# A two-layer hybrid attention step on one core: waits moved in seven stages, and column sums of layer 0 taken on 64 rows per head and divided by quarters

## The chip, the core and the metric

The kernel runs on one core of a Trainium2 chip. The metric is the device time of one execution in microseconds (us). A core has five engines with a queue of instructions each, which run in the order of their queue: TensorE (PE in the rows, with PEld for its weight loads), VectorE (DVE), ScalarE (ACT), GpSimd (POOL) and SyncE (SP, which issues transfers here). Data lie in SBUF and results of matmuls in PSUM, which this kernel uses as eight banks of 128 partitions by 512 floats.

## The reference

Two residual layers are computed for one prompt of 128 tokens and for one sample of 1024 tokens with 1024 channels. Each layer is the same frame around a mixer:

```python
h = pre_norm(x, g_pre, mod)              # rms norm, scale and shift from silu(cond) @ w_mod
y = mixer(h)                             # h @ w_in, branches, gates, concat, @ w_out
x = x + mod[2] * rms_norm(y, g_post)
```

Layer 0 has attention with 8 query heads and 2 key heads of 64 channels (branch A, keys of 128 cached tokens and the sample's 1024), and means over windows of tokens (branch B):

```python
q, k = axial_rope(rms_norm(q)), axial_rope(rms_norm(k))
p = softmax(q @ concat([ctx_k, k]).T * 64 ** -0.5)        # 1152 keys
o_a = p @ concat([ctx_v, v])
y = concat([o_a * silu(ga), pool(u) @ b_map * silu(gb)]) @ w_out
```

Layer 1 has attention over a neighbourhood of tokens plus the cache (branch C, 8 heads) and attention with latent keys and values (branch D, 8 heads, 96 channels for scores: `qd = rms_norm(cq) @ w_uq`, `kv = ckv_all @ w_ukv`), gated and joined in the same way. The outputs are both residual streams and the prompt's keys, values and latents.

## The kernel before

All instructions are written out in order in Python; no scheduler moves them. What decides the order is `weave` (L27): it takes a list of main steps and a list of fill steps, each with a cost in ns that the author gave, runs the main steps in turn, and puts in a fill step whenever the share of fill cost issued lags behind the share of main cost (times `frac`). A step issues all its instructions at once, on several engines. `merge` mixes two fill lists.

Products of float32 are made from two parts: a rounded high part (`whi`, `hTh`, `KH`, made by ACT) and the rest (`wlo`, `hTl`, `KL`, made by DVE or POOL as a subtraction from the same source). PSUM has two pools of banks: three banks A (scores) and five banks B (everything else; `kn.B`, `kn.C`). A matmul that begins a new group waits for a free bank, that is, for the engine which reads the group that lay there.

The stages are these, in order of time:

- The q projection of layer 0 (some 71 to 143 us). `q_main(0)` and `q_main(1)` are its two halves of 256 columns: groups of 48 matmuls in a bank `qkv`, each followed by `q_evac` (squares on ACT, reduction, reciprocal, product and rotation on DVE and POOL). Beside the first half go the keys: `kv1` (norm), `kv2` (rotation) and `kv3` (transposes into a bank `kT`, high part by ACT casts, low part by DVE subtractions) for key groups 0 and 1 (512 tokens each) and 2 (prompt and cache). The shift and scale of layer 1 (`modps`) lie there too.
- The gates and the B branch: twelve weight chunks, each loaded, split into `whi`/`wlo`, and multiplied in a bank `gate`. `pool_mixer` makes the window means `ps` on POOL and DVE, and ACT takes their high part `dh`.
- Attention A: sixteen units in the whole kernel have the form of class `Unit`, eight of them here (four pairs of heads by two halves of 512 queries) and eight in D. A unit first needs the row maxima: 24 matmuls `mp` (`mpiece`), each reduced by DVE (`mx`), one reduction `ms`, eight 1-row matmuls `mT` which turn `ms` into rows (`mrows`), and copies of these rows by ACT into one partition of `QM`. Then for nine key tiles kt and two heads: scores `st`, exponentials `P` by ACT, sums of `P` over key tiles `acc` by POOL (DVE in the last unit of A), and products `pv` in groups after kt 3, 5 and 8 and at the start of the next unit. `fin` ends a unit during the next one: gate times `pv`; `ColSums` makes the column sums `sum` (four matmuls on 32 rows), reciprocals of two halves `srow` (DVE), their two parts `Rhl` (ACT, then DVE), a spread to all rows `rb` by matmuls, and DVE multiplies the gated values `oT` by `rb`. `run_units` weaves the units: the main list is the scores, with the last unit's end and `side` steps at given kt; the fill is the next unit's maxima and the preparation of the unit after (`prep`, with `split_heads`: ACT high part `QP`, DVE low part, ACT copy `QM`, all read from one bank `qT`).
- The output projection of layer 0 with the norms of layer 1 (`outproj`), then attention C (eight heads; `k_split` makes keys `cKH`, `cKL`; the scores `cS` lie in banks A and are read by a DVE operation whose rows bear the name `cmx`), attention D (weights `uq`, `uk` loaded per pair of heads and split; prompt steps `dk`, `dsp`), and the output projection of layer 1.

## Time and profile before

| what | value |
|---|---|
| median of 3 runs (lowest to highest) | 1601.55 us (1599.77 to 1605.28) |
| the profiled execution's own time | 1600.49 us |
| its span, first to last instruction | 1598.7 us |
| mean granted TensorE clock, as a share of 2.4 GHz | 0.980 |
| PE busy | 1518.5 us, 95% |
| DVE busy | 793.5 us, 50% |
| ACT busy | 649.4 us, 41% |
| POOL busy | 625.0 us, 39% |
| DMA queue of the loads, share of 16 engines | 21.7% |

The busy times are sums over one execution of one core. The span is the profile's own measure from the first to the last instruction, and the execution's time has 1.8 us more around it. In rows of the timeline the first number is the start in us from the span's start, the second how long the row's instructions took from the first one's start to the last one's end, and the square bracket at the end tells how long the engine was idle before the row and who released it.

### The profile page before, as it was taken

To read this page: it belongs to the slowest core of one execution; us is meant where nothing else is said; L and a number is where in the kernel's file an instruction comes from. 1 tells how busy PE (TensorE), PEld (TensorE's weight loads), DVE (VectorE), ACT (ScalarE), POOL (GpSimd) and SP (SyncE) were. 2 spreads that over 40 slices of the span, in tenths; PEclk is the share of its full clock that TensorE was granted. 3 is DMA by queue.
4 is the path that set the end of the run, shared out by engine and by line. 5 is a ranking of instruction groups with operands and counts; after the bars stand their busy time and mean duration, and the time that the engine had idled before them with its cause. 6 is when DMAs were issued, how large, how long until landed. Compare 5 with 4: busy or idle time off the path is not lost. (4 is left out here: it accounts for less than half of the span.)

```text
span 1598.7 us, 23592 instructions
## 1 busy us (share of the span) xinstructions
PE 1518.5 (95%) x9095; PEld 1238.9 (77%) x9095; DVE 793.5 (50%) x1776; ACT 649.4 (41%) x1379; POOL 625.0 (39%) x499
## 2 busy tenths in 40 slices
PE   7989999989899999899999999999999999899998
PEld 5978998945555588898989898999976656565786
DVE  4565233357575555534354443423574555546633
ACT  4332211255555323445454544444454434444311
POOL 1743212058669323641303103001256556556421
PEclk8989999999999999999999999999999999999999
DMA  9352104120001232410403130131000000013241
GB/s 343 91 195 81 40 27 145 45 100 14 1 14 40 66 106 80 87 39 15 98 16 75 39 75 24 36 100 58 1 18 21 14 27 15 21 42 117 97 147 53
DMA packets 114080, 104.81 MB, mean 66 GB/s; under 512 B 41776, under 2 KB 99952, under 8 KB 113968
## 3 DMA queue, kind: packets, MB, share of 16 engines
q1 hardware_dynamic: 113792, 103.23, 21.7%
q8 instruction: 72, 1.18, 0.3%
q14 instruction: 40, 0.33, 0.1%
q10 hardware_dynamic: 176, 0.07, 0.0%
HBM read 87.54 MB, written 15.75 MB: 65 GB/s over the span
## 5 line engine op out<-in xcount | busy, mean ns | idle before, releaser
L948 DVE TENSOR_REDUCE mx<-mp 128x1 f32<-128x384 f32 x384 | 189.1, 548 | 99.4 <-PE mp L97 98.0
L124 POOL TENSOR_TENSOR acc<-acc,P 128x1024 f32<-128x1024 f32 x84 | 199.7, 2378 | 75.0 <-ACT P L980 70.0
L980 ACT ACTIVATE P<-st 128x512 f32<-128x512 f32 x256 | 147.2, 598 | 149.1 <-PE st L97 144.1
L124 POOL TENSOR_TENSOR wlo<-raw,whi 128x1024 fp32r<-128x1024 f32 x36 | 87.5, 2433 | 266.5 <-ACT whi L113 153.2
L97 PE MATMUL yps<-whi,ohl 128*128 128x512 f32 x576 | 182.8, 393 | 0.3 <-POOL ohl L124 0.3
L97 PE MATMUL cg<-hT1h,whi 128*128 128x384 f32 x480 | 170.3, 355 | 1.9 <-DVE hf L133 1.2
L97 PE MATMUL cg<-hT1h,wlo 128*128 128x384 f32 x480 | 163.4, 341 | 1.9 <-POOL wlo L124 1.9
L97 PE MATMUL cg<-hT1l,whi 128*128 128x384 f32 x480 | 162.9, 339 | 0.0
L97 PEld LDWEIGHTS yps<-whi,ohl 128*128 128x128 f32 x576 | 108.1, 188 | 25.2 <-issue 2.4
L97 PE MATMUL yps<-wlo,ohl 128*128 128x512 f32 x288 | 112.2, 389 | 0.0
L97 PE MATMUL gate<-hTh,whi 128*128 128x384 f32 x288 | 98.1, 341 | 4.2 <-ACT whi L113 4.2
L97 PE MATMUL gate<-hTh,wlo 128*128 128x384 f32 x288 | 97.8, 340 | 1.3 <-DVE wlo L121 1.3
L97 PE MATMUL gate<-hTl,whi 128*128 128x384 f32 x288 | 97.5, 339 | 0.0
L97 PEld LDWEIGHTS cg<-hT1h,whi 128*128 128x128 f32 x480 | 91.3, 190 | 6.6 <-issue 3.3
L97 PEld LDWEIGHTS cg<-hT1h,wlo 128*128 128x128 f32 x480 | 91.2, 190 | 2.2 <-POOL wlo L124 2.2
L1547 ACT ACTIVATE cs<-cs,cnm 128x640 f32<-128x640 f32 (+1 forms) x64 | 54.8, 857 | 91.9 <-DVE cnm L131 90.9
L97 PEld LDWEIGHTS cg<-hT1l,whi 128*128 128x128 f32 x480 | 91.4, 190 | 0.4
L124 POOL TENSOR_TENSOR acc<-P 128x1024 f32<-128x1024 f32 x14 | 33.6, 2398 | 102.3 <-ACT P L980 101.7
L113 ACT CAST whi<-raw 128x1024 fp32r<-128x1024 f32 (+2 forms) x60 | 61.9, 1037 | 24.1 <-DMA raw<-in_w_in_e 11.0
L97 PE MATMUL pv<-P,dV 128*64 128x512 f32 x288 | 71.4, 622 | 0.2
L97 PE MATMUL st<-QP,KH 128*128 128x512 f32 x144 | 61.8, 429 | 6.6 <-ACT P L980 3.8
L97 PE MATMUL mp<-KH,QP 128*128 128x384 f32 x192 | 57.3, 357 | 6.8 <-DVE msp L1156 2.2
(417 smaller groups left out, 3561.5 us busy)
## 6 DMA issues: line engine op xcount, KB each, us to landing
raw<-in_w_in_o SPq DMA_DIRECT2D x20, 512.0 KB, 4.0
raw<-in_w_in_e SPq DMA_DIRECT2D x18, 512.0 KB, 7.2
wmb<-in_w_mod SPq DMA_DIRECT2D x16, 512.0 KB, 8.4
wm<-in_w_mod SPq DMA_DIRECT2D x16, 512.0 KB, 6.5
wg<-in_w_mod SPq DMA_DIRECT2D x16, 512.0 KB, 4.6
x<-xr SPq DMA_DIRECT2D x9, 512.0 KB, 2.8
xr<-x SPq DMA_DIRECT2D x9, 512.0 KB, 4.8
xn<-in_x_sample SPq DMA_DIRECT2D x8, 512.0 KB, 7.1
```

The source lines that it names most:

```text
L97: self.nc.tensor.matmul(out=out, lhsT=l, rhs=r, start=st, stop=sp)
L113: self.nc.scalar.copy(out=out, in_=in_)
L124: self.nc.gpsimd.tensor_tensor(out=out, in0=a, in1=b, op=op)
L948: kn.nc.vector.tensor_reduce(out=self.mx[:, h, t, c:c + 1], in_=b, axis=AX.X, op=ALU.max)
L980: kn.nc.scalar.activation(out=P[:, h], in_=a, func=AF.Exp, scale=self.scale)
L1547: nc.scalar.activation(out=s[:, 0:n], in_=s[:, 0:n], func=AF.Exp, bias=nm, accum_out=sm)
```

## The change

It has nine parts.

1. In the q projection, only key group 0 is rotated and transposed in the first half; `kv2` and `kv3` of groups 2 and 1 move to the second half. The prompt's keys get a tile `kp` of their own.
2. In the chunks of the B gate, the first step of the weight stream (the next chunk's cast) goes ahead of `pool_mixer`.
3. In all sixteen units the maxima are written to columns 0, 32, 64 and 96 of a zeroed tile of 128x2x97; two matmuls (97 rows each) take the place of eight 1-row ones, and four ACT copies of 1x2x128 that of two of 1x512.
4. In A, the sums of a unit are two matmuls on 64 rows per head, put directly before the next unit's `pv` group at kt 3; DVE takes the reciprocals of four quarters of 128 columns straight from that bank in steps at kt 4 to 7 (two halves of 256 for the last pair of heads) and multiplies `oT` by them. `Rhl` and `rb` are gone there, and in the prompt of A too. D keeps `ColSums`.
5. `split_heads` issues ACT's `QM` copies ahead of DVE's subtractions.
6. In the last unit of A, the weave's `frac` is 1.0, the gate row `gg` and the split of the first output tile stand elsewhere, and the low parts of the output weights' chunks 6 and 7 go to DVE instead of POOL. In layer 1 the low parts of the last unit's weight chunks go to DVE as well.
7. In C, `k_split` only issues the ACT casts; the subtractions and copies go to a list `LATE`, which the weave issues behind its next step.
8. In D, the load and the split of `uq` come at kt 2 and 6 instead of 4 and 8, and in the order that results the key steps `dk` come one group of scores earlier.
9. The output projection of layer 1 takes its k tiles in the order 0 to 7; the prompt's last steps in A take kt 0 to 2 of unit 5 instead of kt 1, since there are two more of them.

```diff
+LATE = []
+def step(f):
+    late = LATE[:]
+    LATE.clear()
+    f()
+    for g in late:
+        g()
...
 def weave(main, fill, frac=1.0):
...
     for c, f in main:
-        f()
+        step(f)
...
-            fill[i][1]()
+            step(fill[i][1])
...
-    fill = [(1, lambda: kv1(0)), (500, lambda: kv1(2)), (500, lambda: kv1(1)), (800, lambda: kv2(0)), (800, lambda: kv2(2)),
-            (800, lambda: kv2(1)), (2000, lambda: None), (500, lambda: wl.need(1)), (500, lambda: kv3(0)),
-            (500, lambda: None), (500, lambda: kv3(2)), (500, lambda: None), (500, lambda: kv3(1)), (500, lambda: None)]
+    fill = [(1, lambda: kv1(0)), (500, lambda: kv1(2)), (500, lambda: kv1(1)), (1000, lambda: None), (800, lambda: kv2(0)),
+            (500, lambda: None), (500, lambda: wl.need(1)), (1500, lambda: None), (500, lambda: kv3(0)), (1000, lambda: None)]
...
+    fill = merge(fill, [(800, lambda: kv2(2)), (500, lambda: kv3(2)), (800, lambda: kv2(1)), (500, lambda: None), (500, lambda: kv3(1))], 1)
     weave(q_main(1), fill, 0.9)
...
-                fill = pool_mixer(g, *pool, dd) + fill
+                fill = fill[:1] + pool_mixer(g, *pool, dd) + fill[1:]
...
+            if not self.early:
+                self.malloc(kn.nc.gpsimd)
...
+    def malloc(self, eng):
+        self.ms = self.kn.T([128, 2, 97], F32R, tag="ms", bufs=1)
+        eng.memset(f32(self.ms), 0.0)
...
+        kn.nc.vector.tensor_reduce(out=self.ms[:, :, 0:97:32], in_=self.mx, axis=AX.X, op=ALU.max)
+    def mrows(self):
+        kn = self.kn
+        b = kn.B("mT")[:, 0:256].rearrange("p (h q) -> p h q", h=2)
+        for h in range(2):
+            kn.mm(b[0:97, h], self.ms[:, h], kn.negid)
         for t in range(4):
-            kn.mm(b[0:1, 128 * t:128 * t + 128], self.ms[:, h, t:t + 1], kn.negid)
-        kn.acopy(self.mdst(h), b[0:1])
+            kn.acopy(self.mdst(t), b[32 * t:32 * t + 1])
...
+def divide(kn, b, g, parts=4):
+    box = {}
+    n = 512 // parts
+    def part(i):
+        if i == 0:
+            box["r"] = kn.T([128, 512], tag="srow", bufs=1)
+        c = slice(n * i, n * i + n)
+        kn.nc.vector.reciprocal(out=box["r"][:, c], in_=b()[:, c])
+        if i == parts - 1:
+            kn.vtt(g(), g(), box["r"])
+    return [(1, lambda i=i: part(i)) for i in range(parts)]
...
+                if sums:
+                    main.append((1, sums[1]))
+                    sums = None
                 main.append((1, lambda u=u, ks=ks: u.pvs(*ks)))
-        weave(main, fill, frac)
+        weave(main, fill, frac if i + 1 < len(units) or not two else 1.0)
...
 def split_heads(kn, b, QP, QM):
     for h in range(2):
+        kn.acopy(QM[h], b[rs[h]])
+    for h in range(2):
         kn.vtt(QP[h][rs[1 - h]], b[rs[h]], f32(QP[h][rs[h]]), ALU.subtract)
-    for h in range(2):
-        kn.acopy(QM[h], b[rs[h]])
...
+    def sums(self):
+        kn = self.kn
+        self.sb = kn.B("sum")
+        for h in range(2):
+            kn.mm(self.sb[64 * h:64 * h + 64, :], kn.ones, self.acc[:, h, :])
+    def fin(self):
...
+        L = divide(kn, lambda: self.sb, self.gT, 4 if self.p < 3 else 2)
+        if self.last:
+            return [(1, f0), (4000, lambda: None), (960, self.sums)] + L
+        return [(1, f0), (1, lambda: None)] + L + [("sums", self.sums)]
...
-        side.setdefault((u, kt + 3), []).append((1, lambda i=i: wo.split1(i)))
+        side.setdefault((u, kt + 3), []).append((1, lambda i=i: wo.split1(i, i > 5)))
...
-    tail = run_units(kn, units, side, extra={0: kn.mod_gate(1, kn.S, 4), 7: [(18000, lambda: None)] + pre})
+    tail = run_units(kn, units, side, extra={0: kn.mod_gate(1, kn.S, 4), 7: [(6000, lambda: None), pre[0], (12000, lambda: None)] + pre[1:]})
...
+        LATE.append(low)
...
-            side.setdefault((2 * p, 4), []).append((1, lambda q=q: L.load_uq(q)))
-            side.setdefault((2 * p, 8), []).append((1, lambda q=q: L.split_uq(q)))
+            side.setdefault((2 * p, 2), []).append((1, lambda q=q: L.load_uq(q)))
+            side.setdefault((2 * p, 6), []).append((1, lambda q=q: L.split_uq(q)))
```

The lines of the changed file stand 18 and more below those of before, so the same helper reads L121 before and L139 after.

**The q projection.** On DVE, in the first half, from the rotations of the keys to the low parts of two weight chunks (`t` is the rotation's scratch, of `k` or of `q`; `q<-qkv` empties a bank), before:

```order
81 L121 TENSOR_TENSOR t_1006<-k,rtk 128x4x16 x8
82 L526 TENSOR_REDUCE hss<-sq 128x8
83 L140 RECIPROCAL hr<-hd 128x8
84 L121 TENSOR_TENSOR q<-qkv,hr 128x512
85 L121 TENSOR_TENSOR t_1034<-q,rtq 128x8x16 x4
86 L121 TENSOR_TENSOR t_1080<-k,rtk 128x4x16 x8
87 L526 TENSOR_REDUCE hss<-sq 128x8
88 L140 RECIPROCAL hr<-hd 128x8
89 L121 TENSOR_TENSOR q<-qkv,hr 128x512
90 L121 TENSOR_TENSOR t_1117<-q,rtq 128x8x16 x4
91 L121 TENSOR_TENSOR wlo<-raw,whi 128x1024 x2
```

And in the change:

```order
81 L544 TENSOR_REDUCE hss<-sq 128x8
82 L158 RECIPROCAL hr<-hd 128x8
83 L139 TENSOR_TENSOR q<-qkv,hr 128x512
84 L139 TENSOR_TENSOR t_1022<-q,rtq 128x8x16 x4
85 L139 TENSOR_TENSOR t_1065<-k,rtk 128x4x16 x8
86 L544 TENSOR_REDUCE hss<-sq 128x8
87 L158 RECIPROCAL hr<-hd 128x8
88 L139 TENSOR_TENSOR q<-qkv,hr 128x512
89 L139 TENSOR_TENSOR t_1102<-q,rtq 128x8x16 x4
90 L139 TENSOR_TENSOR wlo<-raw,whi 128x1024 x2
```

One rotation of eight instructions (`t<-k`, key group 1) is gone from this stretch, and the other stands one `q_evac` later.

**A unit of attention A.** On DVE, from the maxima of one unit to its `ms`, with the end of the unit before it in between (`oT_2625` are the gated values), before:

```order
253 L948 TENSOR_REDUCE mx<-mp 128x1 x8
254 L121 TENSOR_TENSOR oT_2625<-oT_2625,pv 128x512
255 L948 TENSOR_REDUCE mx<-mp 128x1 x4
256 L1032 RECIPROCAL srow<-sum 128x128
257 L948 TENSOR_REDUCE mx<-mp 128x1
258 L1032 RECIPROCAL srow<-sum 128x128
259 L121 TENSOR_TENSOR Rhl<-srow,Rhl 128x256
260 L948 TENSOR_REDUCE mx<-mp 128x1 x7
261 L121 TENSOR_TENSOR oT_2625<-oT_2625,rb 128x512
262 L948 TENSOR_REDUCE mx<-mp 128x1 x3
263 L953 TENSOR_REDUCE ms<-mx 128x8
```

And in the change:

```order
255 L968 TENSOR_REDUCE mx<-mp 128x1 x9
256 L139 TENSOR_TENSOR oT_2625<-oT_2625,pv 128x512
257 L968 TENSOR_REDUCE mx<-mp 128x1 x5
258 L1051 RECIPROCAL srow<-sum 128x128
259 L968 TENSOR_REDUCE mx<-mp 128x1 x4
260 L1051 RECIPROCAL srow<-sum 128x128
261 L968 TENSOR_REDUCE mx<-mp 128x1 x4
262 L1051 RECIPROCAL srow<-sum 128x128
263 L968 TENSOR_REDUCE mx<-mp 128x1
264 L979 TENSOR_REDUCE ms<-mx 128x2x4
265 L1051 RECIPROCAL srow<-sum 128x128
266 L139 TENSOR_TENSOR oT_2625<-oT_2625,srow 128x512
```

The first reciprocal stands one `mx` later than before; there are four instead of two, the subtraction `Rhl` is gone, and the last product has moved from among the `mx` to behind `ms`, where it reads `srow` in SBUF in place of `rb` in PSUM.

**Attention C.** On DVE, at a call of `k_split` for the last 256 keys (the rows ISA with `cs,cmx` read the scores), before:

```order
584 L1543 ISA cs,cmx<-cS,E,cmx 128x384
585 L1543 ISA cmx 128x1
586 L131 TENSOR_SCALAR cnm<-cmx 128x1
587 L121 TENSOR_TENSOR cKL<-cg,cKH 64x256 x2
588 L121 TENSOR_TENSOR cKLp_5960<-cg,cKHp_7338 64x128
589 L121 TENSOR_TENSOR cKLp_5961<-cg,cKHp_7339 64x128
590 L1541 ISA cs,cmx<-cS,E 128x256
591 L1541 ISA cmx 128x1
592 L1543 ISA cs,cmx<-cS,E,cmx 128x384
593 L1543 ISA cmx 128x1
594 L131 TENSOR_SCALAR cnm<-cmx 128x1
```

And in the change:

```order
589 L1612 ISA cs,cmx<-cS,E,cmx 128x384
590 L1612 ISA cmx 128x1
591 L149 TENSOR_SCALAR cnm<-cmx 128x1
592 L1610 ISA cs,cmx<-cS,E 128x256
593 L1610 ISA cmx 128x1
594 L1612 ISA cs,cmx<-cS,E,cmx 128x384
595 L1612 ISA cmx 128x1
596 L149 TENSOR_SCALAR cnm<-cmx 128x1
597 L139 TENSOR_TENSOR cKL<-cg,cKH 64x256 x2
598 L139 TENSOR_TENSOR cKLp_5852<-cg,cKHp_7230 64x128
599 L139 TENSOR_TENSOR cKLp_5853<-cg,cKHp_7231 64x128
```

The four subtractions stand behind the next pair of score reductions instead of ahead of it.

## Rows read from the trace of the kernel before

**Rows 1.** The page: busy time of PE, share of the span, instructions.
```profile
PE 1518.5 (95%) x9095; PEld 1238.9 (77%) x9095; DVE 793.5 (50%) x1776; ACT 649.4 (41%) x1379; POOL 625.0 (39%) x499
```

**Rows 2.** Waits of PE by releaser: us in total, times, longest.
```profile
PE cS L97 <- DVE cmx L1541: 6.1, 3, 2.0
PE kT L106 <- DVE q L121: 5.6, 1, 5.6
PE dq L97 <- POOL uql L124: 4.4, 3, 1.5
PE st L97 <- ACT P L980: 4.4, 4, 2.9
PE dsp L97 <- DVE dKl L121: 4.3, 2, 2.2
PE gate L97 <- ACT whi L113: 4.2, 2, 2.7
PE mp L97 <- DVE mx L948: 4.1, 6, 1.6
PE st L97 <- ACT Px L980: 2.8, 1, 2.8
PE mp L97 <- DVE msp L1156: 2.2, 1, 2.2
...
PE mT L97 <- DVE ms L953: 2.0, 3, 0.7
```

**Rows 3.** Windows: us; busy time of PE, PEld, DVE, ACT, POOL; clock; DMA.
```profile
100.00:120.00 20.00, 16.13 (x115) 13.85 (x119) 12.40 (x24) 8.27 (x21) 7.53 (x8) 0.77 0.81 273
120.00:140.00 20.00, 20.00 (x171) 15.71 (x164) 12.42 (x24) 4.26 (x10) 9.85 (x11) 1.00 0.19 64
400.00:420.00 20.00, 18.06 (x88) 9.40 (x87) 12.89 (x24) 11.06 (x21) 14.03 (x6) 0.91 0.00 1
```

**Rows 4.** The timeline of DVE in the q projection.
```profile
98.65 2.88 DVE L121 TENSOR_TENSOR wlo<-raw,whi 128x1024 fp32r<-128x1024 f32 x2
```

**Rows 5.** The timeline of ACT in a B gate.
```profile
249.12 1.05 ACT L113 CAST dh<-ps 128x1024 fp32r<-128x1024 f32 x1 [5.30 <-DVE ps L121]
```

**Rows 6.** The timeline of PE and ACT at row maxima of A.
```profile
421.24 0.56 PE L97 MATMUL mpp<-KHp,QPp 128*128 128x128 f32 x4
...
318.49 0.64 PE L97 MATMUL mT<-negid,ms 128*1 128x128 f32 x8
...
319.27 1.05 ACT L113 CAST QM<-mT 1x512 fp32r<-1x512 f32 x2
```

**Rows 7.** The timeline of ACT at one `split_heads`.
```profile
345.27 1.17 ACT L113 CAST QM<-qT 64x512 fp32r<-64x512 f32 x2 [1.46 <-DVE QP L121]
```

**Rows 8.** The timeline of PE: sums, spread and two key tiles' values in A.
```profile
415.18 0.64 PE L97 MATMUL sum<-acc,ones 128*32 128x256 f32 x8
...
431.54 0.63 PE L97 MATMUL rb<-Rhl,oneh 128*128 128x256 f32 x4
...
339.39 1.94 PE L97 MATMUL pv<-P,V 128*64 128x512 f32 x8
```

**Rows 9.** Groups of instructions on DVE: busy us, mean ns; idle before.
```profile
L1032 DVE RECIPROCAL srow<-sum 128x128 f32<-128x128 f32 x34 | 32.0, 945 | 0.0
...
L121 DVE TENSOR_TENSOR Rhl<-srow,Rhl 128x256 fp32r<-128x256 f32 x17 | 19.9, 1168 | 13.8 <-ACT Rhl L113 13.8
...
L121 DVE TENSOR_TENSOR oT<-oT,rb 128x512 f32<-128x512 f32 x8 | 5.4, 680 | 5.7 <-PE rb L97 5.7
```

**Rows 10.** The timeline of DVE and POOL at a division in A.
```profile
422.39 2.46 DVE L121 TENSOR_TENSOR Rhl<-srow,Rhl 128x256 fp32r<-128x256 f32 x1 [2.76 <-ACT Rhl L113]
...
422.21 4.86 POOL L124 TENSOR_TENSOR acc<-acc,Px 128x1024 f32<-128x1024 f32 x2 [3.42 <-ACT Px L980]
```

**Rows 11.** The timeline of ACT near the end of A.
```profile
530.94 0.40 ACT L113 CAST Rhl<-srow 128x256 fp32r<-128x256 f32 x1 [4.67 <-DVE srow L1032]
```

**Rows 12.** The timeline of DVE in C.
```profile
808.26 0.86 DVE L121 TENSOR_TENSOR cKL<-cg,cKH 64x256 fp32r<-64x256 f32 x2 [1.77 <-ACT cKH L113]
```

More of the change, by code (lines that the diff above doesn't have):

```diff
@@ L40, in weave @@
     while i < len(fill):
-        fill[i][1]()
+        step(fill[i][1])
         i += 1
+    flush()
 def merge(a, b, off=0):
@@ L1066, in run_units @@
         main = []
+        sums = tail.pop() if tail and tail[-1][0] == "sums" else None
         for kt in range(u.nkt):
@@ L1178, in s5 @@
                 kn.mm(pv[64 * h:64 * h + 64, 128 * p:128 * p + 128], Vp[:, 64 * kv:64 * kv + 64], X["P"][:, 2 * p + h])
+        Pv = X["P"].rearrange("p (j h) q -> p j h q", h=2)
+        X["s"] = kn.B("sum")
+        for h in range(2):
+            kn.mm(v4(X["s"])[64 * h:64 * h + 64], kn.ones, Pv[:, :, h, :])
         g = kn.oTp[:, 0:4, :]
         kn.vtt(g, g, v4(pv))
-        Pv = X["P"].rearrange("p (c i h) q -> p c h i q", c=2, h=2)
-        X["R"] = ColSums(kn)
-        X["R"].sums(lambda h, c: Pv[:, c, h])
-    def s7():
-        X["R"].spread(kn.oTp[:, 0:4, :].rearrange("p j q -> p (j q)"))
     L = [(440, s1)]
@@ L1235, in post @@
         return kn.post(box[t], gg[t // 8], lambda x, y: put(t, x, y))
-    order = (1, 0)
-    pre = [(600, lambda: gg.append(kn.gg(l, 0))), (1, lambda: load(0)), (1, lambda: load(1))]
-    pre += [(1, lambda q=q: split(0, q)) for q in order]
+    order = (0, 1) if l else (1, 0)
+    ks = [4 * q + i for q in order for i in range(4)]
+    pre = [(1, lambda: load(0)), (600, lambda: gg.append(kn.gg(l, 0))), (1, lambda: load(1))]
+    pre.insert(3 if l else 0, (1, lambda: split(0, order[0])))
+    pre.append((1, lambda: split(0, order[1])))
     def run(wo, fills):
@@ L1410, in k_split, with low @@
             kn.acopy(KH[h][rs[h]], b[rs[h], 0:n])
-        for h in range(2):
-            kn.vtt(KL[h][rs[h]], b[rs[h], 0:n], f32(KH[h][rs[h]]), ALU.subtract)
-        for h in range(2):
-            if pool:
-                kn.nc.gpsimd.tensor_copy(out=KH[h][rs[1 - h]], in_=f32(KH[h][rs[h]]))
-            else:
-                kn.vcopy(KH[h][rs[1 - h]], f32(KH[h][rs[h]]))
+        def low():
+            for h in range(2):
+                kn.vtt(KL[h][rs[h]], b[rs[h], 0:n], f32(KH[h][rs[h]]), ALU.subtract)
+            for h in range(2):
+                if pool:
+                    kn.nc.gpsimd.tensor_copy(out=KH[h][rs[1 - h]], in_=f32(KH[h][rs[h]]))
+                else:
+                    kn.vcopy(KH[h][rs[1 - h]], f32(KH[h][rs[h]]))
+        LATE.append(low)
     def k_load(self):
```

41 lines of the change are left out of this document (22 added, 19 removed).

## The prediction

> **What bounds the kernel now.** I read the page first: PE is busy for 1518.5 of 1598.7 us [rows 1], so the end is set by PE's work and by the 80 us in which it stands. Then the list of PE's waits, which the reader should take as a price list: each row says who is waited for, how often, and the longest of them [rows 2]. Then the view by windows of 20 us, for the clock: at full speed it reads 1.00, and after many of the waits it falls [rows 3]. The window from 100 us has 0.77, which is 20 x 0.23 / 0.5 = 9.2 us at the lower of the two levels (1.2 in place of 2.4 GHz); a window with 0.91, as the one from 400 us, has 3.6 us there, and if PE works through them half, 1.8 us, is lost. Ten windows of that view read 0.91, and in each PE had stood shortly before. So a wait that goes may bring 1.8 us more than its own length, and the last readings were of the timelines, to see what ends each wait. DVE works 12.89 of 20 us in a window of attention A [rows 3]: it has room as an average, and what counts is where in its queue an instruction stands.
>
> **The change part by part.** In each part I say what is saved, the value taken, and both ends.
>
> *Keys in the q projection.* The transposes of key group 1 (`kT`) wait 5.6 us for a bank that DVE's `q` must empty [rows 2], and in DVE's queue a pair of low parts, 2.88 us, stands ahead of it [rows 4]. The change takes that transpose and one rotation out of the first half. Of the 9.2 us at the lower clock at most 5.6 were the wait, so at least 3.6 were work, which lost 1.8 [rows 3]. All of it is 5.6 + 1.8 = 7.4. The low end is that the bank is asked for just afterwards by the next projection group and the 2.88 still stands there: 5.6 - 2.9 = 2.7. The high end charges the whole slow stretch: 5.6 + 4.6 = 10.2. What moves to the second half meets a window in which PE works 20.00 of 20, with DVE at 12.42 and ACT at 4.26 [rows 3]; PE is covered there unless a bank comes free late. I take the 7.4.
>
> *Gates.* PE waits twice for ACT's `whi`, 4.2 in all and 2.7 at the longest [rows 2]: ACT stood for 5.30 us at `dh`, with the next chunk's cast behind it [rows 5]. The cast is now ahead, so 2.7 goes, and with it a drop of the clock, 4.5 together. But its low part now runs on DVE ahead of the chain of `ps`, and the product that needs `dl` comes later; what one low part costs, half of the 2.88 of a pair [rows 4], is 1.4, and twice as much of it as bad end. I take 3.5, ends 1.7 and 4.5.
>
> *Maxima.* Eight 1-row matmuls took 0.64, and two of 128 columns cost 0.28 by the nearest row (four in 0.56) [rows 6]: 0.36 less in sixteen units is 5.8. ACT's copies cost 1.05 for two [rows 6]; four of half the width have no row of their own and cost between 1.05 and 2.1. They lie beside the `pv` products, of which two key tiles take 1.94 [rows 8], except at the first unit of A and of D. The memset of 194 columns on POOL has no row either: nothing if POOL is free at the unit's start, and at most an addition of 1024 columns, 2.43 [rows 10], which only delays `acc`. I take 4, ends 1 and 5.8.
>
> *Sums and division in A.* PE: 0.64 for the sums and 0.63 for the spread go, and two products of 512 columns on 64 rows come, which is half of the 1.94 of four such (eight records, two to a product) [rows 8], 0.97. That is 0.3 in eight units and the prompt, 2.7; the first sums wait for nothing new, so 2, ends 0 and 2.7. DVE: two more reciprocals at 0.945 are 1.9, `Rhl` at 1.17 goes, and the product by `srow` costs what the one by `rb` did, 0.68, or as much as `Rhl` did at its worst, 2.46 [rows 9, 10]. Eight units lie between the first maxima at 318 and the cast at 531 us [rows 6, 11], some 26 us each, in which DVE works about 16.8; that grows by 0.7 to 2.5. It lies behind scores and `mx`; uncovered it would stop the maxima. I charge 1.5 for all of A; none of it is the good end, and the bad end is a rival below.
>
> *Order of `split_heads`.* ACT no longer waits 1.46 for DVE between its two pairs [rows 7], and PE's longest wait for `P`, 2.9, lay behind just that [rows 2]; with its clock 4.7, of which I take 2. DVE's subtractions start one pair of copies, 1.17, later, and behind them in the queue stand the `mx` that free banks for `mp`. In seven preparations that is up to 8.2; the wait for `mx` of 1.6 [rows 2] grows surely, the others partly. I charge 3. Together -1, ends +4.7 and -8.2.
>
> *The stall for `msp`.* It waits 2.2 [rows 2] because `Rhl` took 2.46 beside POOL's `acc` [rows 10]. `Rhl` goes, but other work of the prompt comes: 1.5, ends 0 and 4.
>
> *End of A.* `st` waits 2.8 for `Px` [rows 2], since ACT stood 4.67 us for `srow` [rows 11], which DVE made behind its own `acc`. Without `Rhl` on ACT nothing stands there: 2.8 and 1.8 for the clock; DVE gets two low parts more. I take 4, ends 2 and 4.6.
>
> *Attention C.* Three waits of 2.04, 6.1 in all [rows 2]: DVE idles 1.77 for ACT's cast and only then subtracts, with the score reductions queued behind, and PE needs the bank that they read [rows 12]. With the subtractions one step later this goes, and two of the three had a drop of the clock behind them (the windows from 900 and 980 are among the ten), 3.6. The subtractions must still be there before the next scores on these keys. I take 7, ends 5 and 9.7.
>
> *Attention D.* `uql` on POOL stands two additions of `acc` earlier; the three waits for it are 4.4, of which 3.5 should go. `ms` (2.0) comes free earlier with `dKQ`: 1.5. `dKl` (4.3) [rows 2] has one group of scores, about 0.7, more time in two places: 1. Together 6, ends 3 and 10.7. The rest (weights on DVE in the last units, the order of the output's k tiles) lies under PE's work: nothing.
>
> Sum: 7.4 + 3.5 + 4 + 2 - 1.5 - 1 + 1.5 + 4 + 7 + 6 = 32.9. The profiled execution took 1600.49, so 1567.6. The median shown is 1.1 higher; I go up by half of that, to 1568.
>
> **The rivals.**
>
> *The division is held up by POOL.* Each product of `oT` by `srow` takes 2.46 in place of 0.68, as `Rhl` did when it began just after POOL's addition [rows 10]; in seven units (the eighth has no `acc` on POOL) that is 12.5 on DVE, with the next `QP` and `mx` behind it. If PE sees all of it in place of the 1.5 charged, the time is 1578.6. For it: `Rhl` took 1.17 in the mean for 256 columns [rows 9]. Against: the product stands behind `ms`, when the maxima of the unit are done. The Trainium skill, "SBUF — State Buffer", section "Who interferes with whom", states that a VectorE instruction with two SBUF inputs fully blocks against a GpSimd instruction that reads SBUF, and one with at most one SBUF input doesn't. By that, the old product, with one operand in PSUM, was free of it, the new one is not, and the time would be that of this rival; the trace agrees as far as the old product has 0.680 in the mean and `Rhl` 2.46 [rows 9, 10].
>
> *The late `QP` costs in all seven preparations.* PE stands 1.17 in each and loses 1.8 of clock behind it: 20.8 in place of 3, which gives 1585.4. For it: `mp` waits for `mx` six times already, 4.1 in all [rows 2]. Against: the six are 0.7 in the mean.
>
> *The waits come back one step later.* Keys at 2.7, gates at 1.7, C at 5, D at 3, end of A at 2, and the `msp` stall stays: 15.0 less, 1582.6. For it: in each of these places the engine that was late keeps its work. Against: most of it is moved behind work that PE can do meanwhile.
>
> *Slower than before: a bank short in A.* The bank of the sums is now held from kt 3 until the last quarter at kt 7, four of nine key tiles, beside `pv` and `qT`, out of five banks. If `mp` then stands twice in each of seven units as long as its longest wait now, 1.6, with 1.8 of clock, that is 14 x 3.4 = 48 and the time 1615.6. It decides from 33 / 7 = 4.7 us per unit. Against: all waits of `mp` for `mx` together are 4.1 now [rows 2], and the maxima of a unit have 26 us.
>
> *No change that shows.* The first three together come to 46 and can be had in part: 1596 to 1606.
>
> **How the numbers follow.** Forecast (1550 to 1576) 0.61, a little below 1550 within it 0.05; held up by POOL 0.10; late `QP` 0.08; waits come back 0.08; no change 0.07; slower 0.06. Within 0.3%, or 4.8 us, a measurement of this kernel can hardly be told from no change. So faster 0.87, same 0.07, slower 0.06. The range runs from 1550, past the three rivals on the fast side, to 1592, and leaves out 0.05 below and 0.13 above.
>
> **What the profile after would show.** Right: no wait of `kT` for `q` and a clock near 1.00 in the window from 100 us; no waits of `cS` for `cmx` and none of `dq` for `uql`; ACT without a wait inside `split_heads`; two `mT` per unit at about 0.3. Wrong: products of `oT` by `srow` above 2 us with `mp` waiting behind; more waits of `mp` for `QP` and `mx` than now; gate products waiting for `dl`; as many windows at 0.91 as before. The prediction fails most if the seven units of A get longer, since a loss there counts seven times.

## The result: faster by 13 us, where 32.9 were forecast

| | before | changed |
|---|---|---|
| median (lowest to highest) of 6 runs each, us | 1600.4 (1599.27 to 1605.28) | 1587.3 (1586.16 to 1593.61) |
| profiled execution, us | 1600.49 | 1590.44 |
| its span, us | 1598.7 | 1588.6 |
| mean granted clock | 0.980 | 0.978 |

The ratio is 0.9919 (interval 0.9904 to 0.9934): 0.8% faster. The sign was right and the time lies in the range, but 20 of the 32.9 us did not come. Neither did the clock: of a mean of 0.980, 1598.7 x 0.020 / 0.5 = 64 us were at the lower level before, and 1588.6 x 0.022 / 0.5 = 70 us are now. These are single executions: the mean clock was 0.975 to 0.984 in the runs of the kernel before beside the experiments and 0.976 to 0.982 in the six of the changed kernel, so the total did not move clear of that scatter.

The page of the changed kernel answers to [rows 1]: PE is as busy as before, DVE a little more.

```profile
PE 1517.0 (95%) x8927; PEld 1234.9 (78%) x8927; DVE 803.0 (51%) x1788; ACT 654.9 (41%) x1402; POOL 613.6 (39%) x508
```

The list of PE's waits answers to [rows 2] (us in total, times, longest):

```profile
PE mp L115 <- DVE mx L968: 6.1, 10, 1.1
PE gate L115 <- ACT whi L131: 4.9, 1, 4.9
PE st L115 <- ACT P L1008: 4.5, 4, 1.7
PE mp L115 <- DVE QP L139: 4.2, 4, 2.6
PE kT L124 <- POOL kp L142: 4.1, 1, 4.1
PE mp L115 <- DVE dKl L139: 3.6, 4, 1.3
PE kT L124 <- POOL k L142: 2.9, 1, 2.9
...
PE st L115 <- ACT QH L131: 1.8, 1, 1.8
...
PE mp L115 <- DVE QPp L139: 1.6, 1, 1.6
...
PE cS L115 <- DVE cmx L1610: 1.3, 3, 0.5
...
PE st L115 <- ACT QM L131: 1.3, 1, 1.3
```

The reader should see two lists in one. Gone, as forecast, are the waits for `uql`, `Px` and `msp`, and `cS` for `cmx` fell from 6.1 to 1.3. New are `kT` for POOL, `mp` for `QPp` and `dKl`, and `st` for `QM`; `mp` for `QP` grew from 1.9 to 4.2 and `st` for `QH` from 0.5 to 1.8; the gate's wait for `whi` is one of 4.9 where there were two of 4.2 together.

Where the time went is seen best stage by stage. A stage's length is the difference between the starts of its first matmul and of the next stage's in the timeline of PE (us, profiled executions; the units of A and D begin with their first `st`). The four last columns are experiments told below: part 1 undone, part 5 undone, part 1 half undone and 5 undone, and the last version.

| stage | before | changed | e1 | e2 | e9 | e15 |
|---|---|---|---|---|---|---|
| q projection | 71.6 | 71.7 | 71.6 | 71.6 | 68.2 | 68.2 |
| gates and B | 176.3 | 177.7 | 172.5 | 177.7 | 171.3 | 172.0 |
| A, unit 0 | 33.8 | 35.6 | 34.6 | 35.6 | 35.4 | 33.7 |
| A, units 1, 2 (each) | 25.3 | 25.7 | 25.7 | 24.8 | 24.8 | 24.8 |
| A, unit 3 | 36.3 | 34.8 | 32.1 | 30.4 | 30.4 | 31.8 |
| A, units 4 to 6 | 75.9 | 79.6 | 79.6 | 77.4 | 77.4 | 77.4 |
| A, unit 7 | 26.1 | 21.5 | 21.4 | 21.5 | 21.5 | 21.5 |

The scores of C, in four parts, took 89.2, 90.2, 91.8 and 144.7 us before and 89.2, 88.7, 88.6 and 140.8 after: 8.6 less. The eight units of D took 312.7 and now take 313.3. So C alone carries most of the gain, A is even (222.7 to 222.9), and the first 320 us lost a little.

Each of these lengths is from one execution, and stages of the same code differ from kernel to kernel: the gates took 176.3 before and 178.0 in e8, and D took 310.0 to 316.6 in the nine kernels that have the changed kernel's D. Units 1 and 2 of A agree within 0.1 where nothing that they use was edited.

### The profile page after: what moved, and what is told of

It is laid out like the page before. It is cut to its first block, busy times and chain, and to the rows that moved or that the text cites. A ratio compares the mean times of both kernels' runs of the same rounds, so it can differ in the third digit from the quotient of the medians.

```text
span 1588.6 us, 23314 instructions
## 1 busy us (share of the span) xinstructions
PE 1517.0 (95%) x8927; PEld 1234.9 (78%) x8927; DVE 803.0 (51%) x1788; ACT 654.9 (41%) x1402; POOL 613.6 (39%) x508
## 3 DMA queue, kind: packets, MB, share of 16 engines
q8 instruction: 70, 1.15, 0.3%
## 4 chain that ended last, share of the span: by engine, by line
PE 80%; DVE 8%; ACT 6%; POOL 3%; issue 2%; DMA 1%; SPq 0%; ACTq 0%; DVEq 0%; POOLq 0%
PE cg L115 15%; PE yps L115 11%; PE st L115 10%; PE gate L115 8%; PE pv L115 8%; PE lat L115 4%; PE mp L115 4%; PE cpv L115 3%; PE cS L115 2%; PE cT L124 2%; PE dq L115 2%; DVE mx L968 2%; PE qkv L115 1%; PE kv L115 1%; PE modps L115 1%
## 5 line engine op out<-in xcount | busy, mean ns | idle before, releaser
L142 POOL TENSOR_TENSOR wlo<-raw,whi 128x1024 fp32r<-128x1024 f32 x30 | 72.0, 2401 | 247.5 <-ACT whi L131 172.3
L115 PE MATMUL mp<-KH,QP 128*128 128x384 f32 x192 | 61.3, 382 | 9.6 <-DVE QP L139 4.2
L139 DVE TENSOR_TENSOR wlo<-raw,whi 128x1024 fp32r<-128x1024 f32 (+2 forms) x30 | 38.4, 1288 | 61.4 <-ACT whi L131 56.0
L115 PE MATMUL st<-QH,dKh 96*128 96x512 f32 x144 | 63.5, 441 | 2.2 <-ACT P L1008 2.2
```

Source lines behind the costliest of these rows:

```text
L115: self.nc.tensor.matmul(out=out, lhsT=l, rhs=r, start=st, stop=sp)
L139: self.nc.vector.tensor_tensor(out=out, in0=a, in1=b, op=op)
L142: self.nc.gpsimd.tensor_tensor(out=out, in0=a, in1=b, op=op)
```

## The experiments

Each kernel is the changed one with an edit undone or altered, unless said otherwise; `+` and `-` are against the changed kernel. Each group of four shared the runs of the kernel before on their chip; its median was 1601.25, 1601.96, 1601.06 and 1604.78 in the four groups, so across groups the ratios are what to compare; 0.001 of a ratio is 1.6 us. Where a difference of medians is given, the one by ratio stands beside it if the two differ by more than 1 us. `...` marks lines of an edit that are left out.

**e1: part 1 undone** (`kv2` and `kv3` of groups 2 and 1 back in the first half of the q projection).

```diff
...
-            (500, lambda: None), (500, lambda: wl.need(1)), (1500, lambda: None), (500, lambda: kv3(0)), (1000, lambda: None)]
...
+            (800, lambda: kv2(1)), (2000, lambda: None), (500, lambda: wl.need(1)), (500, lambda: kv3(0)),
+            (500, lambda: None), (500, lambda: kv3(2)), (500, lambda: None), (500, lambda: kv3(1)), (500, lambda: None)]
...
-    fill = merge(fill, [(800, lambda: kv2(2)), (500, lambda: kv3(2)), (800, lambda: kv2(1)), (500, lambda: None), (500, lambda: kv3(1))], 1)
```

> The changed kernel with part 1 undone: all three key groups are rotated and transposed in the first half of the q projection again (only the prompt's tile of its own stays). Theory 1 (the waits only came back elsewhere): the waits of kT for POOL (2.9 and 4.1 us) go, the old wait of kT for DVE's q (5.6) and that of qkv (1.3) return, so the q projection stays at 71.6 +- 1; the first loads of the gates are issued 2 us earlier, and the wait of gate for whi at 155 us falls from 4.9 to about 1.6, with 3.4 us less at the lower clock: some 3 to 5 us faster than the changed kernel, 1582 to 1585. Rival (the move as such brings its 7.4 and something else hides it): slower by 7, about 1594.

Measured: 1585.86 us, ratio 0.9901 (0.9883 to 0.9919), 1.4 below the change, 2.9 by ratio, which the intervals don't tell apart. The profile tells more. `kT` waits 5.7 for `q` again, and no longer 2.9 and 4.1 for POOL; the q projection is as long as in both other kernels. The gates take 172.5 in place of 177.7. Two rows of its list of waits:

```profile
PE kT L124 <- DVE q L139: 5.7, 1, 5.7
...
PE gate L115 <- ACT whi L131: 1.8, 1, 1.8
```

So part 1 exchanged its waits for others in its own stage, and cost 3 to 5 us in the next: the five kernels with all of part 1 undone have 172.5 to 174.1 there, the seven of this document that keep it 177.0 to 177.8.

**e2: part 5 undone** (`split_heads` in its old order).

```diff
     for h in range(2):
-        kn.acopy(QM[h], b[rs[h]])
-    for h in range(2):
         kn.vtt(QP[h][rs[1 - h]], b[rs[h]], f32(QP[h][rs[h]]), ALU.subtract)
+    for h in range(2):
+        kn.acopy(QM[h], b[rs[h]])
```

> The changed kernel with part 5 undone: DVE's subtractions of split_heads come before ACT's QM copies again. Theory 2 (the late QP costs more in A than ACT's earlier copies give): the waits of mp for QP (4.2) and QPp (1.6) fall to 1.9 and 0, units 0, 3 and 4 get shorter, and the kernel is 2 to 5 us faster than the changed one, 1582 to 1585. Rival (the order pays): the wait of st for P grows to 2.9 again and the kernel is 2 to 5 us slower, 1589 to 1592.

Measured: 1580.85 us, 0.9867 (0.9854 to 0.988): 6.5 less than the change, 8.3 by ratio. Units of A take 214.3 in place of 222.9. First the timeline of DVE in the changed kernel, in an ordinary unit, then that of PE:

```profile
359.19 1.39 DVE L139 TENSOR_TENSOR QP<-qT,QP 64x512 fp32r<-64x512 f32 x2 [2.27 <-ACT QM L131]
360.61 4.74 DVE L968 TENSOR_REDUCE mx<-mp 128x1 f32<-128x384 f32 x10
```
```profile
360.73 1.40 PE L115 MATMUL mp<-KH,QP 128*128 128x384 f32 x3
361.97 0.39 PE L115 MATMUL st<-QP,KH 128*128 128x512 f32 x1
```

And the same two timelines with part 5 undone, DVE and then PE:

```profile
357.96 1.39 DVE L139 TENSOR_TENSOR QP<-qT,QP 64x512 fp32r<-64x512 f32 x2 [1.08 <-ACT QP L131]
359.39 0.56 DVE L968 TENSOR_REDUCE mx<-mp 128x1 f32<-128x384 f32 x1
360.11 4.27 DVE L968 TENSOR_REDUCE mx<-mp 128x1 f32<-128x384 f32 x9 [0.17 <-PE mp L115]
```
```profile
360.55 0.69 PE L115 MATMUL mp<-KH,QP 128*128 128x384 f32 x3
361.24 0.50 PE L115 MATMUL st<-QP,KH 128*128 128x512 f32 x1
```

DVE is released by `QM` and not by `QP`, so its subtraction starts 1.23 us later; the `mx` behind it are late, and a row of three `mp` lasts 1.40 in place of 0.69. That is no wait that the list of waits could name, since it lies inside one row; with smaller ones after it units 1 and 2 are 0.94 and 0.91 longer. In unit 0 and unit 3, where PE has nothing else to do, the same delay is a full wait (2.6 in place of 1.4 for `QP`, 1.6 for `QPp`), and unit 3 is 4.4 longer. The old order has its price too: `st` waits 6.5 in all for `P`, 3.0 at the longest, against 4.5 and 1.7.

**e3: part 7 undone** (`LATE.append(low)` becomes `low()`).

> The changed kernel with part 7 undone: k_split issues its subtractions at once again. Theory 3 (nearly all that the change gained was gained in attention C): the three waits of cS for cmx return at 2.0 each with drops of the clock, C gets 8 to 9 us longer, and the time is 1595 to 1597. Rival (C's gain came from the earlier stages' shift of the clock's drops): less than 4 us slower.

Measured: 1596.56 us, 0.9964 (0.9952 to 0.9976): 9.3 more, 7.2 by ratio; C is 9.2 longer. Its list of waits has the three old ones back, and two windows of C their lower clock:

```profile
PE cS L115 <- DVE cmx L1610: 6.2, 3, 2.1
```
```profile
900.00:920.00 20.00, 19.36 (x138) 18.20 (x139) 9.55 (x39) 10.84 (x23) 2.40 (x1) 0.91 0.11 30
980.00:1000.00 20.00, 17.59 (x111) 16.61 (x110) 10.06 (x36) 9.99 (x22) 1.88 (x5) 0.91 0.02 4
```

The same two windows of the changed kernel:

```profile
900.00:920.00 20.00, 20.00 (x166) 18.50 (x166) 8.59 (x36) 10.61 (x22) 2.40 (x1) 1.00 0.11 30
980.00:1000.00 20.00, 19.54 (x149) 18.18 (x148) 11.06 (x46) 12.00 (x27) 3.78 (x5) 1.00 0.12 32
```

**e4: part 4 undone in the units of A** (they use `ColSums` again; the prompt keeps the division by quarters).

> The changed kernel with part 4 undone in the units of A (ColSums again: four sums on 32 rows, Rhl, spread; the prompt's division stays new). Theory 4 (the new division is worth its 0.3 us of PE per unit and the end of A, and the longer products of oT by srow, 1.5 in the mean, are covered): the wait of st for Px near the end of A (2.8) returns and A is 3 to 7 us longer, 1590 to 1594. Rival (the division that POOL holds up is what ate A's gain): A gets shorter by 3 or more.

Measured: 1604.73 us, 1.0017 (0.9999 to 1.0034), 17 more than the change, 16 by ratio. That is far more than the theory's 3 to 7. Part of it is the mixture: unit 5 is 4.0 longer than in the changed kernel, and it isn't so in e16. There the prompt's division uses the one tile `srow` that `ColSums` uses as well; that this tile is the reason is read from the code. So this run does not price part 4; e16 undoes all of it.

**e5: parts 1 and 5 undone** (the diffs of e1 and e2 together).

> The changed kernel with parts 1 and 5 undone together. If the loss of the keys' move (gates 5.2 us longer in the profile) and that of split_heads' order (A 8.5 longer) are separate, the gates take about 172.5 us and units 0 to 7 of A as long as with part 5 alone undone, and the time is 1576 to 1580. Rival: one of the two gains was an accident of where the clock's drops fell, and the time stays at 1581 or above.

Measured: 1578.05 us, 0.9856 (0.9835 to 0.9877); A 214.2, gates 173.7. Undoing both gives 9 us of median back.

**e6: part 3 undone** (four-column `ms`, eight 1-row `mT`, two copies).

```diff
...
-        return L + [(300, self.mprep)], [(220, self.mrows)]
+        return L + [(300, self.mprep)], [(220, lambda: self.mrows(0)), (220, lambda: self.mrows(1))]
...
```

> The changed kernel with part 3 undone: eight 1-row matmuls and two copies per unit again. Theory (PE saves 0.33 in each of sixteen units, but the four copies, 1.49 instead of 1.05, are waited for in the first units of A and D): units in the middle get 0.2 to 0.4 longer, units 0 of A and D 1.5 to 2 shorter, in all 0 to 3 us slower, 1587 to 1590. Rival (the copies hurt in all units): faster by 3 or more.

Measured: 1591.01 us, 0.9932 (0.9918 to 0.9946): 3.7 more by medians and 2.1 by ratio, which the intervals don't tell from nothing; 4 were forecast. Units 1 and 2 of A are 0.26 longer each, as the theory had it, and A's first unit is only 0.5 shorter.

**e7: part 8 undone** (`uq` at kt 4 and 8).

> The changed kernel with part 8's kt 4 and 8 again for the load and the split of uq. Theory (the waits of dq for uql, 4.4, have been paid back by P standing behind uq's cast and by dKl): units 1, 3 and 5 of D get 1.5 to 3 longer each and units 0, 2 and 4 get 1 to 3 shorter each, the time is within 3 us of the changed kernel. Rival (part 8 is worth its 4 and what made D's even units longer is something else): 4 or more slower, 1591 and above, with the even units unchanged.

Measured: 1592.6 us, 0.9946 (0.993 to 0.9962): part 8 is worth 5.3 by medians, 4.3 by ratio. The wait of `dq` for `uql` is back with 4.8, three times. The units moved as the theory had it (1, 3 and 5 of D are 3.7, 1.1 and 3.9 longer, 0, 2 and 4 are 1.6 to 2.0 shorter), but the time is the rival's: D is 3.5 longer in all.

**e8: the kernel before with part 7 alone.**

> The kernel before with part 7 alone. Theory (C's gain needs nothing else of the change): attention C, from its first scores to the first dq, gets 8 to 9 us shorter, and the time is 1591 to 1593. Rival: less than 5 us.

Measured: 1593.4 us, 0.9948 (0.9932 to 0.9965), 8.6 less than before. Part 7 is worth the same alone and in the change.

**e9: part 5 undone, part 1 half** (groups 0 and 2 as before the change, group 1 early in the second half).

```diff
...
+            (800, lambda: None), (2000, lambda: None), (500, lambda: wl.need(1)), (500, lambda: kv3(0)),
+            (500, lambda: None), (500, lambda: kv3(2)), (500, lambda: None), (500, lambda: None), (500, lambda: None)]
...
+    fill = merge(fill, [(800, lambda: kv2(1)), (800, lambda: None), (500, lambda: kv3(1)), (3000, lambda: None)], 1)
...
```

> The changed kernel with part 5 undone and the keys arranged anew: groups 0 and 2 are rotated and transposed in the first half at their places of before, and only group 1, early in the second half. Theory (the wait of 5.6 was a shortage of banks made by three key transposes within 14 us, and the change's version lost it again because it also put the rotations late, so that kT waited for its data): no wait of kT above 1 us, the q projection takes 65 to 68 us instead of 71.6, the gates' first wait for whi is 1.6 as before and the gates take about 172.5, and the time is 1571 to 1576. Rival (a bank is short at the next projection group all the same): the projection stays at 70 to 72 and the time at 1577 to 1580.

Measured: 1574.13 us, 0.9833 (0.9821 to 0.9846); q projection 68.2, gates 171.3. The bank's wait is gone, one of 3.2 for POOL's `k` stays, which the theory did not have, and `whi` holds the gates for only 1.6. So 3.4 of the 7.4 could be had, and the gates needn't pay for it.

**e10: parts 1 and 5 undone, and an empty step of cost 220 behind `mrows`**, so that the later steps of D stand where they stood.

> The changed kernel with parts 1 and 5 undone and an empty step of 220 put behind mrows in the main list, so that the weave of each unit has as many steps and as much cost as before. Theory (D's even units got longer because the weave's total shrank and the key and prompt steps moved by a group of scores): units 0, 2, 4 and 6 of D together get 3 to 5 us shorter, and the time is 1573 to 1575. Rival (the place of these steps doesn't matter): D stays within 1 us.

Measured: 1577.2 us, 0.9855 (0.984 to 0.9871). By ratio it is as fast as e5 (0.9856), and D took 310.8, 311.2 in e5: no gain of 3 to 5 shows. This theory fell, as far as a D that scatters by 6 from profile to profile can tell.

**e11: parts 1 and 5 undone, the old maxima in the first unit of A and of D**, where nothing covers the copies.

> The changed kernel with parts 1 and 5 undone, and in the first unit of A and of D the old maxima (eight 1-row matmuls, two copies). Theory (ACT's four copies, 1.49 instead of 1.05, are waited for only there): the wait of st for QM at unit 0 of A (1.3) and for QH at unit 0 of D (1.8) fall by 0.5 to 1 each, time 1576 to 1577.5. Rival: no difference within 1 us.

Measured: 1577.14 us, 0.9859 (0.9844 to 0.9875). A's first unit goes from 35.4 to 33.7, D's from 36.7 to 39.5 with a stretch at the lower clock; e9, which leaves D's first unit as it is in the change, has 39.9 there, so that is not the edit's. No difference in the time.

**e12: part 4 undone in the units of A, part 5 undone.**

> The changed kernel with parts 4 and 5 undone together. Theory (the old division cost 17 us with the new order of split_heads because QP then stands behind it; with the old order the new division is worth 6 to 9): units 0 to 7 of A take 222 to 226 us together instead of the 214.3 with part 5 alone undone, and the time is 1587 to 1590. Rival (the division is worth 14 or more in either order): 1595 or above.

Measured: 1599.31 us, 0.9977 (0.9962 to 0.9991). Unit 5 is again 4.9 longer than with part 5 alone undone: the mixture again, and no price of part 4.

**e13: e9 with the old maxima in the two first units.**

> The arrangement of the keys of e9, the old order of split_heads, and the old maxima in the first unit of A and of D together, all else as in the change. Theory (the three repairs add up): 1571.5 to 1574. Rival (the repairs overlap in the clock's drops): 1574 to 1577.

Measured: 1575.24 us, 0.9812 (0.979 to 0.9834). By its ratio 0.2% under e9; the intervals overlap.

**e14: e13 with the old maxima in all of D.**

> e13 with the old maxima in all units of D. Theory (in D the four copies on ACT and the shorter main list cost more than the 0.33 us of PE per unit give): D's units get 2 to 4 us shorter together, time 1569 to 1572. Rival (the new maxima pay in D as in A): 1 to 3 us slower than e13.

Measured: 1574.94 us, 0.9822 (0.9804 to 0.9839); D 314.6 against 316.2. By ratio it is no faster than e13: undoing the new maxima did not bring D back. This theory fell too.

**e15: e13 with the split of `uq` at kt 7.**

```diff
-            side.setdefault((2 * p, 6), []).append((1, lambda q=q: L.split_uq(q)))
+            side.setdefault((2 * p, 7), []).append((1, lambda q=q: L.split_uq(q)))
```

> e13 with the split of uq at kt 7 instead of 6. Theory (at kt 6 the cast waits for DVE's copies of uqr with P behind it on ACT, 1.7 us at unit 0, and a step later they are done): units 0, 2 and 4 of D get 1 to 2 us shorter each, dq waits for uql less than 0.5, time 2 to 5 us below e13. Rival (one step later POOL's acc stands before uql again): dq waits 1 or more again and the time is 2 to 4 us above e13.

Measured: 1567.43 us (1565.16 to 1571.05), 0.9778 (0.9758 to 0.9798): faster than the changed kernel, and 2.2% faster than before. D took 307.2. It is 7.8 below e13 where 2 to 5 were expected, but the two intervals overlap a little, and the profiled execution is the fastest of its four, as e13's is the slowest of its five. The view of clocks has 0.990 in place of the changed kernel's 0.978, which is 31 us at the lower level (0.983 to 0.990 in the four runs):

```profile
core 0: 1563.4 us, clock 0.990
```

In the changed kernel ACT comes to the cast of `uq` while DVE is still at its source, and stands; the exponentials are queued behind it. ACT and then PE there:

```profile
1196.66 0.83 ACT L131 CAST uqh<-uqr 128x768 fp32r<-128x768 f32 x1 [1.45 <-DVE uqr L136]
1197.51 2.25 ACT L1008 ACTIVATE P<-st 128x512 f32<-128x512 f32 x4
```
```profile
1198.16 0.50 PE L115 MATMUL st<-QH,dKh 96*128 96x512 f32 x1 [1.71 <-ACT P L1008]
```

The timeline of ACT in e15 at the same place:

```profile
1175.78 1.15 ACT L1019 ACTIVATE P<-st 128x512 f32<-128x512 f32 x2
1177.31 0.83 ACT L131 CAST uqh<-uqr 128x768 fp32r<-128x768 f32 x1 [0.38 <-DVE uqr L136]
```

Two exponentials now go ahead of the cast, and PE no longer waits there. But at the end of D's unit 4 the cast stands again, and PE waits for the `QH` behind it, which it did not in e13. ACT and then PE in e15:

```profile
1344.41 0.83 ACT L131 CAST uqh<-uqr 128x768 fp32r<-128x768 f32 x1 [2.77 <-DVE uqr L136]
```
```profile
1347.79 0.50 PE L115 MATMUL st<-QH,dKl 97*128 97x512 f32 x1 [2.07 <-ACT QH L131]
```

Against e13, unit 0 of D is 2.0 shorter and unit 5 is 3.9 longer; units 2 and 4 are 4.8 shorter each, with the same waits in them. PE's waits in D come to 13.9 us in all, against 13.6 in e13 (sums over the timeline of PE). What differs is the clock: by windows of 20 us D spent 7 us at the lower level, and 28 in e13. So the theory named the wait that went, and not the gain.

**e16: all of part 4 undone, the prompt's division too, with parts 1 and 5 undone.**

> The changed kernel with parts 1 and 5 undone and the whole of part 4 too, the prompt's division included. Theory (the division is worth the end of A and the stall for msp, and next to nothing in ordinary units): units 1 and 2 of A as in e5 within 0.2, unit 3 some 4 and unit 7 some 4 to 6 us longer, unit 5 unchanged, in all 9 to 12 us above e5, 1587 to 1590. Rival (17 us as e4 and e12 have it): unit 5 is 5 longer as well, 1594 or more.

Measured: 1581.37 us, 0.9871 (0.9851 to 0.9891), 3.3 above e5 by medians and 2.4 by ratio (it ran in another group), where 9 to 12 were expected; the intervals overlap. In the stage lengths part 4 is worth 7.3 of A: 3.8 in unit 3 and 6.3 in unit 7, less 2.1 in unit 5 and 0.8 in unit 0, and nothing in units 1 and 2. The list of waits of e16 shows the two that part 4 took away:

```profile
PE st L115 <- ACT Px L1008: 4.3, 1, 4.3
...
PE mp L115 <- DVE msp L1203: 2.2, 1, 2.2
```

## Why: each step of the prediction

| term | forecast | measured | by |
|---|---|---|---|
| keys | 7.4 | 0 in its stage | stage length |
| gates | 3.5 | -1.3; 3.9 with part 1 undone, 5.0 with half of it | stage length, e1, e9 |
| maxima | 4 | 3.7 (2.1 by ratio), not told from 0 | e6 |
| sums, division, `msp`, end of A | 6 | 3.3 (2.4 by ratio), not told from 0; 7.3 in stage lengths | e16 against e5 |
| `split_heads` | -1 | -6.5 (-8.3 by ratio) | e2 |
| C | 7 | 8.6 to 9.3 (7.2 to 8.3 by ratio) | e3, e8 |
| D | 6 | -0.6; part 8 alone 5.3 (4.3 by ratio) | stage length, e7 |

By stages, with half of the maxima in A and half in D, 7.4, 3.5, 7, 7 and 8 us were forecast for the q projection, the gates, A, C and D. The two profiles give -0.1, -1.3, -0.2, 8.6 and -0.6, and 3.6 in the rest, for which nothing was forecast.

**Keys: the step that failed first.** The prediction removed the 5.6 because one transpose and one rotation left the first half, and said of the rest "PE is covered there unless a bank comes free late". It asked about banks only, and the data were late. Group 0's rotation too stands one `q_evac` later, and POOL, which makes a part of each rotation, is the last to finish `k`. The timeline of POOL, then that of PE:

```profile
90.99 1.31 POOL L142 TENSOR_TENSOR t<-k,rtk 128x512 f32<-128x512 f32 x1
93.47 1.26 POOL L142 TENSOR_TENSOR k<-t,t 128x512 f32<-128x512 f32 x1 [1.17 <-DVE t L139]
```
```profile
94.78 1.11 PE L124 MATMUL kT<-ident,k 128*128 128x128 f32 x4 [2.90 <-POOL k L142]
```

The group `kp` then waits 4.1 in the second half. Together 7.0 of new waits stand for 6.9 of old ones, the 5.6 [rows 2] and one of `qkv` just ahead of it, in the list of waits of before:

```profile
PE qkv L97 <- DVE q L121: 1.3, 1, 1.3
```

The two signs set down for this stage came out one each way: `kT` waits no more for `q`, but the window from 100 us reads 0.91, not near 1.00.

**Gates: right in itself, and overrun by part 1.** Early in the gates PE now stands 4.9 for `whi`. The timeline of SP, in which the cause stands, SP's list of waits from 140 to 152 us, and the timeline of ACT:

```profile
150.28 0.38 SPq L127 DMA_DIRECT2D bmr<-in_b_map  x1
...
151.80 6.87 SPq L127 DMA_DIRECT2D raw<-in_w_in_e  x4
```
```profile
SPq L127 <- DVE q L139: 20.9, 1, 20.9
SPq L127 <- POOL up L913: 1.1, 1, 1.1
```
```profile
158.77 1.04 ACT L131 CAST whi<-raw 128x1024 fp32r<-128x1024 f32 x1 [9.86 <-DMA raw<-in_w_in_e]
```

`bmr` is a constant of the B branch; in the code its tile is the first of a pool that is opened when the q projection's pool is closed. SP's queue stood with it until DVE and POOL were done with the q projection; the weights `raw` are queued behind. With more work of DVE and POOL at that stage's end it was issued at 150.28, with part 1 undone at 147.47, and the weights at 149.05 instead of 151.80. The stretch from 160 us then ran at a mean clock of 0.84, where before it had 1.00:

```profile
160.00:180.00 20.00, 19.75 (x95) 19.11 (x96) 7.49 (x11) 6.53 (x13) 3.56 (x7) 0.84 0.19 55
```

That part 1 causes the delay is shown by e1 and e9; which of its instructions held `bmr` is only read from this list. With part 1 undone the gates take 172.5 to 174.1 in five kernels, against 176.3 and 178.0 (e8) with the gates of before, so 2.2 to 5.5 came of the term of 3.5; no run undoes part 2 alone.

**Maxima, C: right in mechanism; the size is shown for C.** The two `mT` take 0.31 in place of 0.64 [rows 6], 0.28 were forecast:

```profile
1198.97 0.31 PE L115 MATMUL mT<-negid,ms 128*97 128x128 f32 x2
```

Only at the first units, as the prediction set apart, the four copies show: 1.49 where two took 1.05 [rows 6], and `st` waits 1.3 for `QM`:

```profile
320.03 1.49 ACT L131 CAST QM<-mT 1x256 fp32r<-1x256 f32 x4
```

**Division: the rival was right about the duration, and wrong about the path.** The last product cost DVE 1.516 in the mean, between the 0.68 taken and the 2.46 of the rival. The timeline of DVE has all eight; one of each kind, and the group's row:

```profile
L139 DVE TENSOR_TENSOR oT<-oT,srow 128x512 f32<-128x512 f32 x8 | 12.1, 1516 | 0.3
```
```profile
379.13 1.15 DVE L139 TENSOR_TENSOR oT<-oT,srow 128x512 f32<-128x512 f32 x1
...
437.63 2.37 DVE L139 TENSOR_TENSOR oT<-oT,srow 128x512 f32<-128x512 f32 x1
...
540.73 0.69 DVE L139 TENSOR_TENSOR oT<-oT,srow 128x512 f32<-128x512 f32 x1
```

Three took 1.15, three 2.36 to 2.58, all six while POOL ran additions `acc`; the last two, with POOL idle, took 0.69. The Trainium skill, "SBUF — State Buffer", section "Who interferes with whom", says that a VectorE instruction with two SBUF inputs contends with a GpSimd instruction that reads SBUF, for ports that are an exclusive lock; the trace agrees: each of the six ended 0.55 us after the addition that ran when it began. For the one of 2.37, in the timeline of POOL:

```profile
437.07 2.38 POOL L142 TENSOR_TENSOR acc<-acc,P 128x1024 f32<-128x1024 f32 x1
```

The rival counted seven such products; there were six. The new `sum` took 1.08 on PE, where 0.97 was estimated. But the six together are 6.6 us above 0.69 on DVE, behind `ms`, and units 1 and 2 were as long with the old sums (24.8 in e16 as in e2). (In DVE's queue as shown ahead of the prediction, 12 `mx` stand ahead of the first reciprocal before and 14 in the change, so it stands two later, not one.) The gains came where the prediction put them, at `msp` and at the end of A.

**`split_heads`: the mechanism named, the size wrong.** The prediction charged 3 for the late subtractions and credited 2 for ACT. The credit is seen (the wait of 2.9 for `P` in unit 0 is one of 1.6); net of it the edit cost 6.5 in the median and 8.5 in the units of A. By windows of 20 us A spent 20 us at the lower level in the changed kernel and 10 in e2, so some 5 of the 8.5 are the clock, by the estimate that half of such time is lost. So the rival of the late `QP` named the loss, and its 20.8 was too much. The step that failed is that waits of `mp` would show as waits: some 0.9 per ordinary unit is lost inside rows.

**D: a third of the forecast came as shorter waits, and the clock took it back.** `dq` for `uql` (4.4) and `mT` for `ms` (2.0) are gone, and the 4.3 of `dsp` for `dKl` is now 3.6 of `mp` for `dKl` [rows 2]; new are 1.7 of `st` for `P`, 1.8 for `QH` (0.5 before) and short ones. Over the timeline of PE the waits in D add up to 16.3 before and 14.1 in the changed kernel, so 2.2 of the 6 came. The new ones are all under 2 us, but the clock fell behind them: by windows of 20 us D spent 7 us at the lower level before and 21 now. If half of such time is lost, D without these drops would be 309 and 303 long. By this estimate D's own work and waits did get 6 shorter, 2.2 by waits and the rest by work such as the `mT`, which the prediction had counted under the maxima; and the clock took it back. The window in which `mp` waits 1.27 for `dKl`, the row of PE first:

```profile
1268.23 0.41 PE L115 MATMUL mp<-dKh,QH 96*128 96x384 f32 x1 [1.27 <-DVE dKl L139]
```
```profile
1260.00:1280.00 20.00, 17.88 (x71) 11.03 (x67) 9.79 (x16) 7.46 (x15) 7.10 (x3) 0.83 0.00 1
```

e10 and e14 tried two causes and brought nothing. In e15 D is 5.5 shorter than before the change (307.2), with 7 us at the lower level in both, which agrees with that estimate. Against e13 it is not the waits that differ. In unit 2, for one, e13 and e15 have the same waits one after the other (0.8 for `mx`, 1.3 and 0.5 for `dKl`, 0.8 between these two for `psum`); here are the windows with the 1.3, e13 first and then e15:

```profile
1240.00:1260.00 20.00, 17.72 (x75) 10.15 (x74) 13.10 (x24) 5.72 (x12) 8.95 (x5) 0.84 0.00 1
```
```profile
1240.00:1260.00 20.00, 17.26 (x86) 12.27 (x84) 13.31 (x25) 9.04 (x18) 7.74 (x4) 1.00 0.05 14
```

Which of the short waits brings the lower clock, and why the same units run at full speed in one version and not in another, stays open.

**Clock, and the sum.** The time lies nearest to two rivals, the late `QP` (1585.4) and the waits that come back (1582.6), and both happened in part. A short bank in A did not show: `mp` waits 6.1 in all for `mx`, 1.1 at the longest, where 48 were priced. The step that failed in the sum is the price of the clock: 1.8 for each wait that goes, of which 4.7 us stand in the 32.9 above the lengths of the waits themselves. In C that came, with 7 us at the lower level before and none now. Elsewhere new waits stood close by: by the same windows A went from 14 to 20 us there and D from 7 to 21. One slip of the sums changes nothing: the first three rivals come to 43.8 together, not to 46.
